# A feed-forward block whose residual adds move to transfers, and a sixth pair of row tiles in seven products

## The chip, the cores and the metric

The kernel runs on one core of one Trainium2 chip. The metric is the device time of one execution in microseconds; three runs of the kernel before gave a median of 1134.25 (1134.21 to 1136.03). A core has a matrix engine (TensorE, PE in the profile; its weight loads are PEld), a vector engine (VectorE, DVE), a scalar engine (ScalarE, ACT), a general engine (GpSimd, POOL) and an engine that issues transfers (SyncE, SP). Matrix products are summed in eight banks (each 128 x 512 float32), from which VectorE and ScalarE read. Everything else lies in on-chip tiles of 128 partitions.

## The reference

One decoder layer on 256 tokens of width 2048, all in float32. The mixers (gated linear attention and sparse attention) come first and give the residual h. The change lies in what follows, the feed-forward part, of width 5632:

```python
h = x + jnp.concatenate([gla_out, nsa_out], axis=-1) @ w_out
m = rms_norm(h, ffn_norm_g)
return h + (jax.nn.silu(m @ w_gate) * (m @ w_up)) @ w_down
```

## The kernel before

**Split products.** Each float32 operand of a large product is split into a rounded high part and a low rest, and a product is three matmuls: high by high, high by low, low by high. `in_parts` (lines 563 to 565) makes the two parts: line 564 copies the high part on ScalarE, line 565 subtracts it from the original on VectorE. Weights arrive as raw tiles of 1 MB (`fraw`, three buffers) by transfers that SyncE issues in `load4` (line 932), and their parts lie in `ftwo` tiles (four buffers, each with high and low part of up to 4 x 128 x 512 numbers).

**Stages.** After the projections, the mixers and the output projection (to about 440 us) the feed-forward part runs in eleven blocks of 512 hidden columns. In each block `gate_up` computes gate and up for both token tiles (t = 0, 1; 128 tokens each), and one block later `down` multiplies the activations by four column groups n of `w_down` and adds the result to the residual tiles `h_sb[n]` (two token tiles of 512 columns each). The order is gate_up(0), gate_up(1), down(0), gate_up(2), down(1) and so on to gate_up(10), down(9), down(10). `down(10)` is the last: it adds in halves of 256 columns and sends each half out.

**Pairs of row tiles.** The 2048 rows of the gate and up weights are 16 tiles of 128, taken in eight pairs (0 to 7). A plain pair is 8 products of 3 matmuls, 24 in all. A pair in `PAIRS7` is computed by a Strassen-like scheme with 7 products, 21 matmuls: the weights are added up first (lines 983 to 985, VectorE), the sums are split too (into a second `ftwo` buffer), and the activations are needed in four combined forms, made once by `pair_forms` after the output projection and kept in a `g4` tile for all blocks. Eight banks hold the sums, numbered 1 to 8. After the last pair of this kind banks 1, 5, 6 and 7 are combined (line 1008 on ScalarE, lines 1009 to 1012 on VectorE), and after the last pair of all the gating follows (lines 1021 to 1024): the sums from banks 2, 3, 4 and 8 are added, ScalarE applies Silu, VectorE multiplies.

**Order of the work.** The program is written in the order of the loops; `drive` interleaves side work (the transposes of the last block's activations, `turn_act`) at a set pace. A planner then orders the instructions of each engine by priority and by its own costs and hands out tile buffers. Each engine works through its own queue in that order, so what stands behind a waiting instruction waits too. Pairs run in `ORDER`: in the first block first 1 and 3, plainly, and then 0, 5, 2, 4, 6, 7; later 0, 1, 2, 4, 3, 5, 6, 7, with 1, 3 and 7 plain.

**Residual adds.** After both token tiles of a column group have been summed over the block, `down` adds them on VectorE, one instruction of 128 x 512 for each token tile (line 1055).

Of the kernel before, what the change touches and what calls it, by code (L numbers as in the profile page):

```python
# [11 lines left out]
AF = mybir.ActivationFunctionType  # L12
ALU = mybir.AluOpType
AX = mybir.AxisListType

P = 128
S = 256
NT = S // P
# [18 lines left out]
def kernel(  # L37
# [4 lines left out]
    nc = tc.nc  # L42
    act, mm = nc.scalar.activation, nc.tensor.matmul
    TT, TS, STT = nc.vector.tensor_tensor, nc.vector.tensor_scalar, nc.vector.scalar_tensor_tensor
# [12 lines left out]
    def slot(pool, tag, bufs, align=None):  # L57
        def f(shape, dt=F32):
            n_tiles[0] += 1
            return pool.tile([P] + list(shape), dt, tag=tag, bufs=bufs, name=f"{tag}_{n_tiles[0]}", align_bytes=align)  # L60
        return f
# [3 lines left out]
    g4, g2, g1, small = slot(gp, "g4", 24, LINE), slot(s2p, "g2", 13), slot(s1p, "g1", 7), slot(s1p, "sm", 12)  # L65

    def bank():
        n_tiles[0] += 1
        return pp.tile([P, 512], F32, tag="bank", name=f"bank_{n_tiles[0]}")
# [36 lines left out]
    last = {}  # L106
# [85 lines left out]
    def transpose(o, i, n=P):  # L192
        return nc.tensor.transpose(o, i, ident[:n, :n])  # L193
# [369 lines left out]
    def in_parts(hi, lo, ps):  # L563
        act(hi, ps, AF.Copy)  # L564
        TT(lo, ps, f32(hi), ALU.subtract)  # L565
# [273 lines left out]
    h_sb = []  # L839
# [22 lines left out]

    PAIRS7, FIRST7 = (0, 2, 4, 5, 6), (0, 2, 4)


    OLD = (1, 3)
    ORDER0, ORDER = OLD + (0, 5, 2, 4, 6, 7), (0, 1, 2, 4, 3, 5, 6, 7)
    forms = {}  # L870
    turned = set()

    def pair_forms(pair, v):

        f = g2([4, P])
        a0, a1, b0, b1 = v[:, 0, :P], v[:, 0, P:], v[:, 1, :P], v[:, 1, P:]
        TT(f[:, 0], b1, a1, ALU.subtract)
        TT(f[:, 1], f[:, 0], b0, ALU.subtract)
        TT(f[:, 2], b0, b1, ALU.subtract)
        TT(f[:, 3], a0, f[:, 1], ALU.add)  # L880
        r = forms[pair] = g4([2, 4, P], F32R)
        in_parts(r[:, 0], r[:, 1], f)
# [32 lines left out]
    rf = kp.tile([P, NT], F32, name="rf")  # L915
    fw = {}

    def ffn_pools():
        nonlocal g2, small
        for pool in (wp, s2p, s1p, cp):  # L920
            pool.release()
        fr = ctx.enter_context(tc.tile_pool(name="fr", bufs=1, reuse_waits="tile"))
        fs = ctx.enter_context(tc.tile_pool(name="fs", bufs=1, reuse_waits="tile"))
        fp = ctx.enter_context(tc.tile_pool(name="fp", bufs=1, reuse_waits="tile"))
        fw["raw"], fw["two"] = slot(fr, "fraw", 3, LINE), slot(fp, "ftwo", 4, LINE)
        g2, small = slot(fs, "f2", 10), slot(fs, "fm", 4)

    def load4(parts):

# [10 lines left out]
    def parts_of(src):  # L940

        if not fw:
            return split(src, 4, 512)
        n = src.shape[1]
        hi, lo = two_parts()
        in_parts(hi[:, :n], lo[:, :n], src)
        return [(hi[:, k], lo[:, k]) for k in range(n)]

    def gate_up(fb, aTs, before):

        hi, lo = g4([4, S], F32R), g4([4, S], F32R)
        aTs.append((hi, lo))
        banks = {}

        def product(q, a, w, k):

            if q not in banks:
                banks[q] = bank()
                new = True
            else:  # L960
                new = False
            for i, (x, m) in enumerate(((a[0], w[k][0]), (a[0], w[k][1]), (a[1], w[k][0]))):
                todo[q] -= 1
                mm(banks[q], x, m, start=new and i == 0, stop=todo[q] == 0)  # L964

        def tokens(k, t):
            assert k in turned
            return tuple(x[k // 4][:, k % 4, t * P:(t + 1) * P] for x in (hT_h, hT_l))

        order, sevens = (ORDER0, FIRST7) if fb == 0 else (ORDER, PAIRS7)  # L970
        last7 = max(sevens, key=order.index)
        todo = dict.fromkeys((1, 5, 6, 7), 3 * len(sevens))
        todo.update(dict.fromkeys((2, 3, 4), 3 * len(sevens) + 6 * (8 - len(sevens))))
        todo[8] = 6 * (8 - len(sevens))
        for at, pair in enumerate(order):
            if fb == 0 and at == len(OLD):
                ffn_pools()
            a, b = 2 * pair, 2 * pair + 1
            r = load4([(m[0], a, 2, fb * FB) for m in (w_gate, w_up)])
            if pair in sevens:  # L980
                w = parts_of(r[:, 0:3])
                s1, s2 = g4([2, 512]), g4([2, 512])
                TT(s1, r[:, 1:3], r[:, 3:4].to_broadcast([P, 2, 512]), ALU.add)  # L983
                TT(s2[:, 0], s1[:, 1], r[:, 1], ALU.add)  # L984
                TT(s2[:, 1], s2[:, 0], r[:, 0], ALU.add)  # L985
                f = [tuple(forms[pair][:, i, j] for i in range(2)) for j in range(4)]
                product(1, tokens(b, 0), w, 1)
                yield 2
                product(2, tokens(a, 0), w, 0)
                yield 2  # L990
                product(3, f[3], w, 2)
                yield 2
                hi_, lo_ = two_parts()
                in_parts(hi_[:, 0:2], lo_[:, 0:2], s1)
                in_parts(hi_[:, 2:4], lo_[:, 2:4], s2)
                w = [(hi_[:, k], lo_[:, k]) for k in range(4)]
                for q, x, k in ((5, f[0], 0), (7, f[2], 1), (6, f[1], 2), (4, tokens(a, 1), 3)):
                    product(q, x, w, k)
                    yield 2
            else:  # L1000
                w = parts_of(r)
                for q, t, m in ((2, 0, 0), (3, 0, 1), (4, 1, 0), (8, 1, 1)):
                    for j in range(2):
                        product(q, tokens(a + j, t), w, 2 * m + j)
                        yield 2
            if pair == last7:
                q1, u, q5u, q7u, q57u = (g2([512]) for _ in range(5))
                act(q1, banks[1], AF.Copy)
                TT(u, banks[6], q1, ALU.add)
                TT(q5u, banks[5], u, ALU.subtract)  # L1010
                TT(q7u, banks[7], u, ALU.add)
                TT(q57u, banks[5], q7u, ALU.subtract)
                if before is not None:
                    urgent.append(before)
        if fb == 0:
            drain(urgent)
            rms(rf, ssh)
            TT(rf, rf, hback, ALU.mult)
        gs = []
        for t, (g, gq, u_, uq) in enumerate(((q1, 2, q5u, 3), (q7u, 4, q57u, 8))):  # L1020
            TT(g, banks[gq], g, ALU.add)
            act(g, g, AF.Silu, scale=rf[:, t:t + 1])
            TT(u_, banks[uq], u_, ALU.add)
            STT(g, u_, rf[:, t:t + 1], g, ALU.mult, ALU.mult)
            gs.append(g)
        turns[fb] = turn_act(gs, hi, lo)

    turns = {}

    def turn_act(gs, hi, lo):  # L1030
        for t in range(NT):
            ts = slice(t * P, (t + 1) * P)
            p = bank()
            for j in range(4):
                transpose(p[:, j * P:(j + 1) * P], gs[t][:, j * P:(j + 1) * P])
                if j % 2:
                    yield
            pv = p.rearrange("p (j s) -> p j s", j=4)
            in_parts(hi[:, :, ts], lo[:, :, ts], pv)

    def down(f0, aTs, last):

        for m in range(2):
            banks = [[bank() for _ in range(NT)] for _ in range(2)]
            for f, (ah, al) in enumerate(aTs):
                end = f == len(aTs) - 1
                for i, n in enumerate((2 * m, 2 * m + 1)):
                    ws = parts_of(load4([(w_down[0], 4 * (f0 + f), 4, n * 512)]))
                    yield from chunk([banks[i]], ah, al, ws, f == 0, end, t_first=last and end)
                    if not end:  # L1050
                        continue
                    for t in range(NT):
                        for c in range(0, 512, 256 if last else 512):
                            cs = slice(c, c + (256 if last else 512))
                            TT(h_sb[n][:, t, cs], banks[i][t][:, cs], h_sb[n][:, t, cs], ALU.add)  # L1055
                            if last:
                                nc.sync.dma_start(out[t * P:(t + 1) * P, n * 512 + c:n * 512 + c + 256], h_sb[n][:, t, cs])


    drive([proj(C_LR, ev_go(0), ((0, 256), (256, 272)), first_chunk)], 2)  # L1060
# [50 lines left out]
```

## Time and profile before

| | |
|---|---|
| median of three runs | 1134.25 us |
| profiled execution | 1134.1 us, its span 1132.4 us |
| busy in the span: PE, DVE, ACT, POOL | 1120.4, 965.9, 619.8, 23.6 us |
| granted TensorE clock | 0.999 of full speed |
| moved by DMA | 213.45 MB, 189 GB/s on average |

The span is that of the profiled instructions; 1.7 us lie around it. "L1055" is line 1055 of the kernel before. A group's row names the operation, output<-input, the partitions x elements, the count, then the busy time, the mean duration and the idle time just before it with what ended that idle time. A row of a timeline has the start, the length, the engine, the line and the operation; "x2" is two instructions merged. The share "DMA" is the mean busy share of the 16 DMA engines.

### The profile page before, as it was taken

The page shows a single profiled execution, that of the slowest core. Times are in us where ns is not written, and L with a number is a line of the kernel's source. Part 1 is how long each engine was busy: PE and PEld are TensorE (multiplying, and loading weights), DVE is VectorE, ACT ScalarE, POOL GpSimd, SP SyncE. Part 2 cuts the span into 40 slices and gives each one's busy share as a digit, 9 for nine tenths or more (in the row PEclk, how much of TensorE's full clock was granted, in tenths as well). Part 3 has the DMA queues.
Part 4 walks back from the last instruction along what each step waited for, and adds up shares of the span by engine and source line. Part 5 has one row for each costly group of instructions (what it writes and reads, how often), then busy time and mean ns, then how long its engine had stood idle before and what let it go on. Part 6 is the DMA issues. An engine that isn't in the chain of part 4 may idle for free.

```text
span 1132.4 us, 14359 instructions
## 1 busy us (share of the span) xinstructions
PE 1120.4 (99%) x5515; PEld 927.1 (82%) x5515; DVE 965.9 (85%) x1205; ACT 619.8 (55%) x763; POOL 23.6 (2%) x53
## 2 busy tenths in 40 slices
PE   9999999999999999999999999999999999999998
PEld 8888889998777777788888888888888888888886
DVE  6547779987588678999999999999999999999993
ACT  7654466544466486664555546364555555464640
POOL 3000000100000000000000000000000000000000
PEclk9999999999999999999999999999999999999999
DMA  7655543445853354556665656555565556565652
GB/s 269 233 186 186 186 149 114 152 151 152 299 182 112 112 186 149 184 193 219 221 224 180 225 180 233 186 202 193 199 208 200 207 166 223 185 243 168 196 211 75
DMA packets 110446, 213.45 MB, mean 189 GB/s; under 512 B 5109, under 2 KB 8217, under 8 KB 110378
## 3 DMA queue, kind: packets, MB, share of 16 engines
q1 hardware_dynamic: 110378, 212.54, 56.1%
q8 instruction: 43, 0.70, 0.2%
q14 instruction: 25, 0.20, 0.1%
HBM read 210.42 MB, written 2.10 MB: 188 GB/s over the span
## 4 chain that ended last, share of the span: by engine, by line
PE 89%; issue 4%; DVE 4%; DMA 1%; POOL 0%; SPq 0%; ACT 0%; POOLq 0%; DVEq 0%
PE bank L261 45%; PE bank L964 37%; PE bank L193 3%; PE bank L817 1%; PE bank L759 1%; DVE ftwo L565 1%; DMA raw<-in_w_out_dram 1%; DVE lo L130 1%; DMA g<-in_x_dram 1%; PE bank L513 1%; DVE g L515 0%; DVE g L518 0%; DVE g L490 0%; PE bank L675 0%; DVE g L489 0%
## 5 line engine op out<-in xcount | busy, mean ns | idle before, releaser
L964 PE MATMUL bank<-ftwo,g 128*128 128x512 f32 x1905 | 444.9, 392 | 1.3 <-DVE ftwo L565 1.1
L964 PEld LDWEIGHTS bank<-ftwo,g 128*128 128x128 f32 x1905 | 354.0, 188 | 75.4 <-DVE ftwo L565 2.2
L261 PE MATMUL bank<-hi,g 128*128 128x512 f32 (+3 forms) x1152 | 326.3, 366 | 0.8 <-DVE g L615 0.6
L564 ACT ACTIVATE ftwo<-fraw 128x1536 fp32r<-128x1536 f32 (+1 forms) x130 | 226.3, 1741 | 141.5 <-PE bank L261 41.2
L565 DVE TENSOR_TENSOR ftwo<-fraw,ftwo 128x1536 fp32r<-128x1536 f32 (+1 forms) x130 | 267.2, 2067 | 13.8 <-ACT ftwo L564 13.8
L261 PE MATMUL bank<-ftwo,g 128*128 128x512 f32 x1056 | 241.9, 389 | 0.0
L261 PEld LDWEIGHTS bank<-ftwo,g 128*128 128x128 f32 x1056 | 198.0, 188 | 41.6 <-DVE g L565 0.4
L261 PEld LDWEIGHTS bank<-hi,g 128*128 128x128 f32 x1152 | 199.3, 189 | 30.9 <-issue 2.3
L130 DVE TENSOR_TENSOR lo<-raw,hi 128x1024 fp32r<-128x1024 f32 (+3 forms) x125 | 151.4, 1218 | 74.5 <-ACT hi L129 74.0
L564 ACT ACTIVATE ftwo<-g 128x1024 fp32r<-128x1024 f32 x106 | 110.5, 1058 | 158.9 <-DVE g L983 75.2
L261 PE MATMUL bank<-lo,g 128*128 128x512 f32 (+1 forms) x576 | 195.3, 365 | 0.5 <-DVE lo L130 0.5
L129 ACT ACTIVATE hi<-raw 128x1024 fp32r<-128x1024 f32 (+3 forms) x125 | 131.3, 1056 | 109.3 <-PE bank L261 77.5
L565 DVE TENSOR_TENSOR ftwo<-g,ftwo 128x1024 fp32r<-128x1024 f32 x106 | 127.2, 1217 | 8.2 <-ACT ftwo L564 8.2
L261 PEld LDWEIGHTS bank<-lo,g 128*128 128x128 f32 x576 | 102.6, 189 | 15.0 <-issue 0.9
L1055 DVE TENSOR_TENSOR g<-bank,g 128x512 f32<-128x512 f32 (+1 forms) x96 | 59.3, 642 | 15.6 <-PE bank L261 14.7
L983 DVE TENSOR_TENSOR g<-fraw 128x1024 f32<-128x1024 f32 x53 | 64.5, 1216 | 0.0
L564 ACT ACTIVATE g<-bank 128x512 fp32r<-128x512 f32 (+1 forms) x50 | 29.2, 587 | 21.8 <-PE bank L193 12.5
L193 PE MATMUL bank<-ident,g 128*128 128x128 f32 (+2 forms) x214 | 38.4, 278 | 2.4 <-DVE g L548 1.1
L565 DVE TENSOR_TENSOR g<-bank,g 128x512 fp32r<-128x512 f32 (+1 forms) x50 | 33.6, 681 | 7.7 <-ACT g L564 7.4
L193 PEld LDWEIGHTS bank<-ident,g 128*128 128x128 f32 (+2 forms) x214 | 27.5, 142 | 12.3 <-issue 2.3
L985 DVE TENSOR_TENSOR g<-g,fraw 128x512 f32<-128x512 f32 x53 | 36.3, 685 | 0.6
L984 DVE TENSOR_TENSOR g<-g,fraw 128x512 f32<-128x512 f32 x53 | 36.3, 685 | 0.5
(192 smaller groups left out, 639.3 us busy)
## 6 DMA issues: line engine op xcount, KB each, us to landing
fraw<-in_w_down_dram SPq DMA_DIRECT2D x44, 1024.0 KB, 5.1
fraw<-in_w_gate_dram SPq DMA_DIRECT2D x86, 512.0 KB, 3.8
fraw<-in_w_up_dram SPq DMA_DIRECT2D x86, 512.0 KB, 4.7
raw<-in_w_in_dram SPq DMA_DIRECT2D x36, 1024.0 KB, 5.1
raw<-in_w_out_dram SPq DMA_DIRECT2D x16, 1024.0 KB, 5.1
raw<-in_w_in_dram SPq DMA_DIRECT2D x4, 1072.0 KB
g<-in_x_dram SPq DMA_DIRECT2D x7, 512.0 KB, 9.8
raw<-in_w_in_dram SPq DMA_DIRECT2D x3, 1056.0 KB, 11.4
```

The costliest lines, as they stand in the source:

```text
L129: act(h[:, i:i + n], r[:, k + i:k + i + n], AF.Copy)
L130: TT(o[:, i:i + n], r[:, k + i:k + i + n], f32(h[:, i:i + n]), ALU.subtract)
L193: return nc.tensor.transpose(o, i, ident[:n, :n])
L261: last["mm"] = mm(bk[t], a[:, k, t * P:(t + 1) * P], m[:, off:off + w], start=(first_ and k == 0 and i == 0), stop=(end and k == 3 and i = ...
L513: mm(p[:, j * P:(j + 1) * P], u, w, start=True, stop=True)
L564: act(hi, ps, AF.Copy)
L565: TT(lo, ps, f32(hi), ALU.subtract)
L964: mm(banks[q], x, m, start=new and i == 0, stop=todo[q] == 0)
L983: TT(s1, r[:, 1:3], r[:, 3:4].to_broadcast([P, 2, 512]), ALU.add)
L984: TT(s2[:, 0], s1[:, 1], r[:, 1], ALU.add)
L985: TT(s2[:, 1], s2[:, 0], r[:, 0], ALU.add)
L1055: TT(h_sb[n][:, t, cs], banks[i][t][:, cs], h_sb[n][:, t, cs], ALU.add)
```

## The change

Three things are changed together.

1. In `down`, for all blocks but the last, ScalarE copies the two sums of a column group from the banks into a tile `step` (two buffers, 128 x 2 x 512 each), and one transfer issued from GpSimd adds the tile to `h_sb[n]`. VectorE's adds stay only in the last block.
2. From the third block on six pairs (0, 1, 2, 4, 5, 6) are in seven products, with the order 0, 1, 3, 2, 4, 5, 6, 7. The second block has four such pairs (0, 2, 4, 5) in the order 0, 1, 2, 3, 4, 6, 5, 7; the first is as before. `pair_forms` makes the forms of pair 1 as well.
3. The small tiles of the feed-forward part are arranged anew in the same space: in place of ten buffers `f2` of 512 columns there are two `gate` buffers, one `up` buffer (each two token tiles of 512) and the two of `step`. The combined sums are written into parts of `gate` and `up`.

```diff
-    PAIRS7, FIRST7 = (0, 2, 4, 5, 6), (0, 2, 4)
+    PAIRS7, FIRST7 = (0, 1, 2, 4, 5, 6), ((0, 2, 4), (0, 2, 4, 5))
...
-    ORDER0, ORDER = OLD + (0, 5, 2, 4, 6, 7), (0, 1, 2, 4, 3, 5, 6, 7)
+    ORDERS, ORDER = (OLD + (0, 5, 2, 4, 6, 7), (0, 1, 2, 3, 4, 6, 5, 7)), (0, 1, 3, 2, 4, 5, 6, 7)
...
-        f = g2([4, P])
+        f = fw["up"]([4, P]) if fw else g2([4, P])
...
-        g2, small = slot(fs, "f2", 10), slot(fs, "fm", 4)
+        fw["up"], fw["step"] = slot(fs, "up", 1), slot(fs, "step", 2)
+        g2, small = slot(fs, "gate", 2), slot(fs, "fm", 4)
...
-        order, sevens = (ORDER0, FIRST7) if fb == 0 else (ORDER, PAIRS7)
+        order, sevens = (ORDERS[fb], FIRST7[fb]) if fb < 2 else (ORDER, PAIRS7)
...
-                q1, u, q5u, q7u, q57u = (g2([512]) for _ in range(5))
-                act(q1, banks[1], AF.Copy)
-                TT(u, banks[6], q1, ALU.add)
-                TT(q5u, banks[5], u, ALU.subtract)
-                TT(q7u, banks[7], u, ALU.add)
-                TT(q57u, banks[5], q7u, ALU.subtract)
+
+                gate, up = g2([NT, 512]), fw["up"]([NT, 512])
+                act(gate[:, 0], banks[1], AF.Copy)
+                TT(up[:, 1], banks[6], gate[:, 0], ALU.add)
+                TT(up[:, 0], banks[5], up[:, 1], ALU.subtract)
+                TT(gate[:, 1], banks[7], up[:, 1], ALU.add)
+                TT(up[:, 1], banks[5], gate[:, 1], ALU.subtract)
...
+                    if not last:
+                        step = fw["step"]([NT, 512])
+                        for t in range(NT):
+                            act(step[:, t], banks[i][t], AF.Copy)
+                        nc.gpsimd.dma_start(h_sb[n], step, accum_op=ALU.add)
+                        continue
                     for t in range(NT):
-                        for c in range(0, 512, 256 if last else 512):
-                            cs = slice(c, c + (256 if last else 512))
+                        for c in range(0, 512, 256):
+                            cs = slice(c, c + 256)
                             TT(h_sb[n][:, t, cs], banks[i][t][:, cs], h_sb[n][:, t, cs], ALU.add)
-                            if last:
-                                nc.sync.dma_start(out[t * P:(t + 1) * P, n * 512 + c:n * 512 + c + 256], h_sb[n][:, t, cs])
+                            nc.sync.dma_start(out[t * P:(t + 1) * P, n * 512 + c:n * 512 + c + 256], h_sb[n][:, t, cs])
```

More of the change, by code (lines that the diff above doesn't have):

```diff
@@ L1018, in gate_up, with turn_act @@
             TT(rf, rf, hback, ALU.mult)
-        gs = []
-        for t, (g, gq, u_, uq) in enumerate(((q1, 2, q5u, 3), (q7u, 4, q57u, 8))):
+        for t, (gq, uq) in enumerate(((2, 3), (4, 8))):
+            g, u = gate[:, t], up[:, t]
             TT(g, banks[gq], g, ALU.add)
             act(g, g, AF.Silu, scale=rf[:, t:t + 1])
[L1023 to L1026, printed above, removed]
+            TT(u, banks[uq], u, ALU.add)
+            STT(g, u, rf[:, t:t + 1], g, ALU.mult, ALU.mult)
+        turns[fb] = turn_act(gate, hi, lo)
     turns = {}
-    def turn_act(gs, hi, lo):
+    def turn_act(gate, hi, lo):
         for t in range(NT):
@@ L1034, in turn_act @@
             for j in range(4):
-                transpose(p[:, j * P:(j + 1) * P], gs[t][:, j * P:(j + 1) * P])
+                transpose(p[:, j * P:(j + 1) * P], gate[:, t, j * P:(j + 1) * P])
                 if j % 2:
```

## The prediction

> **What bounds the kernel now.** I read the page's busy line first, then the chain that ended last in order of time, then the windows of one block of the feed-forward part, then who waited for whom. The page, and rows of the chain (start, length, engine, line):
>
> ```profile
> PE 1120.4 (99%) x5515; PEld 927.1 (82%) x5515; DVE 965.9 (85%) x1205; ACT 619.8 (55%) x763; POOL 23.6 (2%) x53
> ...
> PE 89%; issue 4%; DVE 4%; DMA 1%; POOL 0%; SPq 0%; ACT 0%; POOLq 0%; DVEq 0%
> ```
>
> ```profile
> 642.48 21.76 PE bank L261 x96
> 664.25 36.04 PE bank L964 x159
> ...
> 705.33 21.76 PE bank L261 x96
> ```
>
> From about 440 us on the chain is TensorE alone, back to back. A block lasts 705.33 - 642.48 = 62.85 us: 96 down products, 177 gate and up products (159 of them in the row shown), eight transposes. One product costs 21.76 / 96 = 0.2267 us. The windows (length, then busy time of PE, PEld, DVE, ACT and POOL, granted clock, DMA share, GB/s) tell how close the others are:
>
> ```profile
> 375.00:440.00 65.00, 64.29 (x302) 51.93 (x301) 43.84 (x71) 46.19 (x76) 1.39 (x2) 1.00 0.46 162
> 440.00:516.80 76.80, 75.45 (x330) 60.34 (x329) 75.93 (x72) 46.43 (x39) 0.00 (x0) 1.00 0.60 201
> ```
>
> ```profile
> 642.40:705.30 62.90, 62.90 (x283) 51.98 (x282) 60.17 (x58) 33.78 (x27) 0.00 (x0) 1.00 0.61 202
> ```
>
> TensorE is never idle in a steady block, at full granted clock. VectorE is second, 60.17 of 62.90 us: 2.7 us free. ScalarE has 29 us free and GpSimd all. VectorE's waits, summed over nine blocks (516.8 to 1082.7 us), and TensorE's between 380 and 516 us:
>
> ```profile
> DVE ftwo L565 <- ACT ftwo L564: 18.8, 32, 1.2
> ```
>
> ```profile
> PE bank L964 <- DVE ftwo L565: 1.1, 2, 0.8
> ```
>
> VectorE's idle time is no lateness of its own: it waits for ScalarE's first half of a split, and ScalarE, as shown below, waits for TensorE to give a split buffer back. So TensorE bounds, and a product removed is worth 0.2267 us as long as VectorE keeps its lead.
>
> **The change, part by part.** *Products on TensorE.* A pair of row tiles takes 24 products plainly and 21 in seven products. From the third block on six pairs of eight are in seven, before five: 3 fewer in each of 9 blocks. The second block has four pairs where it had five: 3 more. The first keeps its three. Together 27 - 3 = 24 products, 24 x 0.2267 = 5.44 us off TensorE. The down product's matmuls stay.
>
> *VectorE.* Its groups in the block 642.4 to 705.3 us (instructions, busy us, mean ns):
>
> ```profile
> L565 DVE TENSOR_TENSOR ftwo<-fraw,ftwo 128x2048 fp32r<-128x2048 f32 x7 | 16.0, 2284 | 1.0 <-ACT ftwo L564 1.0
> L565 DVE TENSOR_TENSOR ftwo<-g,ftwo 128x1024 fp32r<-128x1024 f32 x10 | 11.9, 1216 | 1.2 <-ACT ftwo L564 1.2
> L565 DVE TENSOR_TENSOR ftwo<-fraw,ftwo 128x1536 fp32r<-128x1536 f32 x5 | 8.7, 1750 | 0.3 <-ACT ftwo L564 0.3
> L983 DVE TENSOR_TENSOR g<-fraw 128x1024 f32<-128x1024 f32 x5 | 6.1, 1215 | 0.0
> L1055 DVE TENSOR_TENSOR g<-bank,g 128x512 f32<-128x512 f32 x8 | 5.3, 685 | 0.2
> L985 DVE TENSOR_TENSOR g<-g,fraw 128x512 f32<-128x512 f32 x5 | 3.4, 686 | 0.1
> L984 DVE TENSOR_TENSOR g<-g,fraw 128x512 f32<-128x512 f32 x5 | 3.4, 684 | 0.0
> ```
>
> A pair turned from plain to seven adds 1.750 + 2 x 1.216 + 1.215 + 0.684 + 0.686 - 2.284 = 4.48 us; the eight residual adds taken away give 8 x 0.685 = 5.48. Net -1.0 by means; consecutive instructions overlap by some 0.08 us (two of 1.216 last 2.35 in the timeline below), which makes it -0.76. So 59.4 us of work stand in a block of 62.90 - 0.68 = 62.2 us: 2.8 us free, as now. VectorE doesn't become the bound on average.
>
> *ScalarE.* Its groups in the same block:
>
> ```profile
> L564 ACT ACTIVATE ftwo<-fraw 128x2048 fp32r<-128x2048 f32 x7 | 13.4, 1917 | 4.8 <-DMA fraw<-in_w_down_dram 2.3 <-PE bank L964 1.3 <-PE bank L261 1.1
> L564 ACT ACTIVATE ftwo<-g 128x1024 fp32r<-128x1024 f32 x10 | 10.4, 1059 | 15.9 <-PE bank L964 8.9 <-DVE g L983 5.8 <-DVE g L985 1.1
> L564 ACT ACTIVATE ftwo<-fraw 128x1536 fp32r<-128x1536 f32 x5 | 7.4, 1489 | 7.9 <-PE bank L261 3.5 <-issue 2.9 <-PE bank L964 0.8
> ...
> L1008 ACT ACTIVATE f<-bank 128x512 f32<-128x512 f32 x1 | 0.6, 580 | 0.0
> ```
>
> The pair adds 1.489 + 2 x 1.059 - 1.917 = 1.69 us, the eight copies from the banks 8 x 0.580 = 4.64 (that row is such a copy). 33.78 + 6.3 = 40.1 of 62.2: free on average. But behind a copy stand ScalarE's splits, and behind those VectorE's and TensorE. So the lead has to be walked.
>
> *The lead in the gate and up stage.* Three timelines (start, length, engine):
>
> ```profile
> 658.89 1.92 ACT L564 ACTIVATE ftwo<-fraw 128x2048 fp32r<-128x2048 f32 x1 [1.12 <-PE bank L261]
> 664.33 1.49 ACT L564 ACTIVATE ftwo<-fraw 128x1536 fp32r<-128x1536 f32 x1 [3.52 <-PE bank L261]
> ```
>
> ```profile
> 664.08 36.21 PE L964 MATMUL bank<-ftwo,g 128*128 128x512 f32 x159
> ```
>
> ```profile
> 676.15 2.35 DVE L565 TENSOR_TENSOR ftwo<-g,ftwo 128x1024 fp32r<-128x1024 f32 x2
> ...
> 679.02 3.95 DVE L565 TENSOR_TENSOR ftwo<-fraw,ftwo 128x2048 fp32r<-128x2048 f32 x2
> ```
>
> There are four split buffers, and both waits end as TensorE finishes a down product (one at 664.08 - 5.44, one at 664.08). Today's tightest place: the fourth and fifth pairs. After pairs of 21, 24 and 21 products TensorE has run 66 x 0.2267 = 14.96 us, so it starts the fourth at 679.04 and, after its 21, the fifth at 683.80; that one's split ends at 679.02 + 2.2 = 681.2: a lead of 2.6 us. Now the new order (pairs 0, 1, 3, 2, 4, 5, 6, 7, with 3 and 7 plain), time from the stage's start, a seven-product pair taking 2.04 us from its first buffer and 2.72 from its second: the four-buffer rule lets pair 1's buffers begin at -5.44 and 0, pair 3's at 2.04, pair 2's at 4.76 and 6.80, pair 4's at 9.52 and 14.96, 5's at 17.0 and 19.7, 6's at 21.8 and 24.5, 7's at 26.5. With ScalarE's and VectorE's times above in that order, VectorE finishes pair 1's second half at 3.2 (4.3 with the last two copies in front; needed at 6.80), pair 3 at 6.2 (7.2; 9.52), pair 4's second half at 18.3 (21.76), pair 6's first and second at 27.0 and 29.3 (29.24 and 31.28), pair 7 at 31.5 (34.0). The lead shrinks to about 2 us where it was 2.6, and stays positive: I book no stall. Were that cover gone, each us of lateness would cost TensorE that us in every block.
>
> *The transfers that add.* Four a block, 40 in all, of 512 KB between on-chip tiles, issued from GpSimd's queue, where nothing else stands after 440 us. No such transfer is in the trace. Nearest rows:
>
> ```profile
> fraw<-in_w_gate_dram SPq DMA_DIRECT2D x86, 512.0 KB, 3.8
> ...
> g<-in_x_dram SPq DMA_DIRECT2D x7, 512.0 KB, 9.8
> ```
>
> ```profile
> GB/s 385 166 42 0 0 0 0 0 0 0 72 102 344 400 415 415 215 15 113 245 396 347 351 359 68 38 0 0 53 143 328 396 415 396 200 0 0 0 0 0
> ```
>
> The last line cuts 642.4 to 664.1 us in 40: loads come in bursts of up to 415 GB/s, with gaps. One transfer read twice (its source and what it adds to) is 1.05 MB, 2.5 us at that rate; four are 10 us of the 0.39 x 62.2 = 24.3 us that the engines have free. From below: nothing, they sit in the gaps. From above: 9.8 us each, 39 us, which overfills the block by 15 us. I take 2.5 to 5 us and no cost, since the gate rows (3.8) carry the same bytes in this very stage, the x rows only at the crowded start. The two copy tiles are reused two products later, 10.9 us: only a transfer beyond some 9 us holds ScalarE back. The last block adds on VectorE again: to each quarter of the residual three down products, 16.3 us, after that quarter's last transfer can start; the tail keeps its length.
>
> *GpSimd beside VectorE.* In the first 10 us the trace shows the two in each other's way:
>
> ```profile
> 6.98 0.44 POOL L347 TENSOR_SCALAR_AFFINE_SELECT lmask<-lmask 128x64 f32<-128x64 f32 x2
> ...
> 7.47 1.28 POOL L347 TENSOR_SCALAR_AFFINE_SELECT lmask<-lmask 128x64 f32<-128x64 f32 x2
> ```
>
> ```profile
> 1.65 1.07 DVE L368 CAST identb<-ident 128x128 bf16<-128x128 f32 x1 [0.46 <-POOL ident masks.py:199]
> ...
> 7.14 1.50 DVE L130 TENSOR_TENSOR lo<-raw,hi 128x528 fp32r<-128x528 f32 x2
> ...
> 17.06 0.28 DVE L367 CAST cneg<-g 128x256 bf16<-128x256 f32 x1
> ```
>
> Two selects take 1.28 us instead of 0.44 beside a two-operand subtraction, which itself isn't slowed (1.50 for two); and a cast takes 1.07, when one twice its size takes 0.28, at the time of GpSimd's long memset. So an issue could cost VectorE anything from 0 to 0.8 us. I take 0: the stage has two-operand operations alone, and beside those GpSimd was the one to wait. The Trainium skill ("SBUF — State Buffer", section "Who interferes with whom") says that a VectorE instruction with two SBUF inputs contends with a GpSimd instruction that reads SBUF, and not with one that only writes it; by that rule writing a transfer's descriptors costs VectorE nothing and the sum stays as it is, by the cast's row it would be the second rival's. The rows of the selects agree with the rule; none here shows an issue from GpSimd.
>
> *The rest, with one answer.* The forms of pair 1, four small subtractions and additions and one split more, fall before 440 us, where VectorE has 65 - 43.8 = 21 us free: 0. The four combinations and the gating keep their operations under other tile names; the single "up" tile is read out a stage before it is written again: 0. One more kept form leaves 24 - 18 = 6 big tiles for two split inputs a pair and two activations: 0. Between 440 and 516.8 us VectorE is full (75.93 of 76.80) and one pair less in the second block takes 4.5 us off it; the 1.1 us that TensorE waited there could shrink; I take 0, because the longer wait stands at the head of that block, before the pair that changes:
>
> ```profile
> 479.75 29.30 PE L964 MATMUL bank<-ftwo,g 128*128 128x512 f32 x127 [0.80 <-DVE ftwo L565]
> ```
>
> **Sum.** The profiled execution took 1134.1 us (span 1132.4), the median 1134.25: the same within 0.02%. 1134.1 - 5.44 = 1128.7 us, 0.5% faster. Below 0.2% (2.3 us) a run can't be told from no change.
>
> **The rivals.**
> (1) *Crowded transfers*, slower. Speaks for it: DMA is 0.61 busy, in bursts; against: 24 us free a block. It decides from 24.3 / 4 = 6.1 us of all engines per transfer; at 6.5 a block grows by 1.7 us, in ten blocks 17: 1128.7 + 17 = 1146; at 9.8 a block grows by 15 us: 1278.
> (2) *GpSimd's issues block VectorE*, slower. With the cast's 0.8 us, 4 x 0.8 = 3.2 against 2.8 free: 0.4 a block, 4 us: 1132.7; from (2.8 + 0.54) / 4 = 0.84 us an issue all the gain is gone, at 1.2 it is 1128.7 + 20 = 1149. For: the cast's row; against: the select's.
> (3) *The lead runs dry*, no change. Should the planner not start pair 1 as early as the walk, the 2 us are overrun and TensorE waits 0.6 us a block: 1134.
> (4) *A copy too early in ScalarE's queue*, slower. A pair of copies queued one product ahead of its sums holds the split behind it for up to 5.44 us, 3.4 more than the lead: ten times is 34 us, 1163; with 3 us it is 1 us a block, 1139. It decides from 2.6 us. For: ScalarE already waits for TensorE's banks; against: VectorE's own adds waited only 0.2 us in the block shown, so the order fits TensorE's pace.
>
> **How the numbers follow.** Forecast 0.60 (own range 1127.5 to 1131.5: a us gained in the second block, a few stalls); crowded 0.13; issues 0.11; lead 0.06; copies 0.10. Faster: 0.60 and a quarter of the issues' 0.11, less what the forecast's upper end loses, 0.61. Same: the lead and some of the issues, 0.08. Slower: the rest, 0.31. The range goes from 1127.3 to 1142: it holds the forecast, the lead, most of the issues and the mild ends of copies and crowding.
>
> **What would show it.** Right: blocks of 62.2 us in the chain, TensorE alone, the second one 0.7 us longer; VectorE's L1055 group left with the last block's 16 halves; ScalarE near 40 us a block; transfers landing within 9 us. Wrong: TensorE waiting for "ftwo" in each block (lead, copies), DMA share near 1 with waits for "fraw" (crowded), VectorE's means above 2.28 and 1.22 us (issues), ScalarE waiting for a transfer out of "step".

## The result, and the profile after

The changed kernel takes 1151.83 us (median of four runs, 1144.97 to 1155.52) against 1135.03 for the kernel before in the same comparison: 1.0141 times, interval 1.0091 to 1.0191. It is slower by about 1.4%, where 0.5% faster was forecast. The profiled execution took 1153.2 us, its span 1151.4, which is 19.0 us more than the span before.

The page of the changed kernel, its busy line, queues, chain and transfers:

```profile
PE 1121.0 (97%) x5491; PEld 919.8 (80%) x5491; DVE 948.1 (82%) x1170; ACT 673.9 (59%) x860; POOL 58.0 (5%) x93
...
q1 hardware_dynamic: 110378, 212.54, 54.3%
q0 software_dynamic: 5760, 20.97, 9.5%
...
PE 51%; DVE 25%; DMA 13%; issue 9%; ACT 1%; SPq 1%; POOL 0%; DVEq 0%; ACTq 0%; POOLq 0%
...
fraw<-in_w_gate_dram SPq DMA_DIRECT2D x86, 512.0 KB, 4.5
fraw<-in_w_up_dram SPq DMA_DIRECT2D x86, 512.0 KB, 5.7
...
g<-step POOLq DMA_DIRECT2D x40, 512.0 KB, 7.6
```

The 24 products are gone (5515 to 5491 matmuls), yet the chain is no longer TensorE's: VectorE has 25% of it and DMA 13%, where they had 4% and 1%. The loads of `w_up` land after 5.7 us instead of 4.7. The new queue q0 carries the transfers that add: they take 9.5% of 16 engines over 1151.4 us, so 109 us for 40, or 2.73 us of all engines each.

Starts of the down products in TensorE's timeline:

```profile
517.36 21.92 PE L261 MATMUL bank<-ftwo,g 128*128 128x512 f32 x96
583.65 22.09 PE L261 MATMUL bank<-ftwo,g 128*128 128x512 f32 x96
...
713.92 22.13 PE L261 MATMUL bank<-ftwo,g 128*128 128x512 f32 x96
776.81 21.99 PE L261 MATMUL bank<-ftwo,g 128*128 128x512 f32 x96
...
903.00 22.21 PE L261 MATMUL bank<-ftwo,g 128*128 128x512 f32 x96
969.52 22.33 PE L261 MATMUL bank<-ftwo,g 128*128 128x512 f32 x96
```

The blocks are not all alike. The three that begin at 517.36, 713.92 and 903.00 last 66.3, 62.9 and 66.5 us; the nine between 517.36 and 1101.58 us last 584.2 together, 24.7 more than nine of the 62.17 that the products alone give. 24.7 - 5.4 saved = 19.3, against 19.0 measured: the whole difference is in these blocks. Who waited for whom from 440 us on, first TensorE, then VectorE:

```profile
PE bank L965 <- DVE ftwo L565: 18.3, 20, 3.0
```

```profile
DVE g L984 <- DMA fraw<-in_w_up_dram: 41.8, 17, 5.3
DVE ftwo L565 <- ACT ftwo L564: 21.1, 14, 3.1
```

TensorE waits for splits, and VectorE, ahead of them, for late loads: line 984 (983 before) is the first sum of a pair's weights. One long block shows the sequence. SyncE, VectorE and TensorE (the gate and up stage starts at 925):

```profile
917.51 1.05 SPq L933 DMA_DIRECT2D fraw<-in_w_up_dram  x1
```

```profile
927.41 1.22 DVE L984 TENSOR_TENSOR g<-fraw 128x1024 f32<-128x1024 f32 x1 [3.84 <-DMA fraw<-in_w_up_dram]
928.67 0.69 DVE L985 TENSOR_TENSOR g<-g,fraw 128x512 f32<-128x512 f32 x1
929.39 0.69 DVE L986 TENSOR_TENSOR g<-g,fraw 128x512 f32<-128x512 f32 x1
930.00 2.35 DVE L565 TENSOR_TENSOR ftwo<-g,ftwo 128x1024 fp32r<-128x1024 f32 x2
934.25 1.23 DVE L984 TENSOR_TENSOR g<-fraw 128x1024 f32<-128x1024 f32 x1 [1.90 <-DMA fraw<-in_w_up_dram]
935.39 3.95 DVE L565 TENSOR_TENSOR ftwo<-fraw,ftwo 128x2048 fp32r<-128x2048 f32 x2
```

```profile
937.73 23.46 PE L965 MATMUL bank<-ftwo,g 128*128 128x512 f32 x102 [2.78 <-DVE ftwo L565]
```

The load issued at 917.51 reaches VectorE 9.9 us later. The sums that need it, those of pair 2, stand at the head of VectorE's queue, and behind them the second half of pair 1 (930.00). In this block that half comes just in time; in the blocks from 583.65, 969.52 and 1035.36 TensorE waits 0.35 to 0.48 us for it. Behind the next late sums (934.25) stands pair 3 (935.39), for which TensorE waits 2.78 us here.

The length of a block follows this wait of VectorE around the end of the down stage. Three more rows, from the blocks that begin at 583.65, 713.92 and 776.81:

```profile
609.25 1.22 DVE L984 TENSOR_TENSOR g<-fraw 128x1024 f32<-128x1024 f32 x1 [5.14 <-DMA fraw<-in_w_up_dram]
...
736.45 1.22 DVE L984 TENSOR_TENSOR g<-fraw 128x1024 f32<-128x1024 f32 x1 [2.03 <-DMA fraw<-in_w_up_dram]
...
798.83 1.23 DVE L984 TENSOR_TENSOR g<-fraw 128x1024 f32<-128x1024 f32 x1 [1.67 <-DMA fraw<-in_w_up_dram]
```

| first wait for the load of pair 2 | 1.67 | 2.03 | 2.55 | 3.40 | 5.14 | 5.26 | 5.28 us |
|---|---|---|---|---|---|---|---|
| length of the block | 62.8 | 62.9 | 63.4 | 64.2 | 66.0 | 65.8 | 66.2 us |

These are the seven blocks with one wait above 1 us; the other two, from 517.36 and 903.00, have a second one and last 66.3 and 66.5. Against the 62.17 us of the products the first 1.0 to 1.6 us of the wait cost nothing; every further microsecond costs about one.

The windows of these microseconds in the block from 903.00, columns as in the prediction:

```profile
914.00:919.40 5.40, 5.40 (x26) 4.46 (x25) 5.37 (x7) 3.12 (x5) 0.86 (x1) 1.00 1.05 290
919.40:924.90 5.50, 5.50 (x26) 4.57 (x25) 2.85 (x3) 2.63 (x4) 0.85 (x1) 1.00 1.05 301
924.90:930.00 5.10, 5.10 (x24) 4.24 (x23) 2.52 (x3) 4.61 (x5) 0.86 (x1) 1.00 1.06 308
```

For 16 us the DMA engines are full (a share above 1 means that the times of packets overlap). In the kernel before their share in the same part of a block, from 11 to 27 us after its start, was

```profile
653.10:669.10 16.00, 16.00 (x73) 13.23 (x72) 15.53 (x17) 7.45 (x6) 0.00 (x0) 1.00 0.55 188
```

so 0.45 x 16.0 = 7.2 us were free, and the four transfers, issued from 7 to 23 us after the start, ask for 4 x 2.73 = 10.9.

### The profile page after: what moved, and what is told of

It is laid out like the page before. It is cut to its first block, busy times and chain, and to the rows that moved or that the text cites. A ratio compares the mean times of both kernels' runs of the same rounds, so it can differ in the third digit from the quotient of the medians.

```text
span 1151.4 us, 14498 instructions
## 1 busy us (share of the span) xinstructions
PE 1121.0 (97%) x5491; PEld 919.8 (80%) x5491; DVE 948.1 (82%) x1170; ACT 673.9 (59%) x860; POOL 58.0 (5%) x93
## 4 chain that ended last, share of the span: by engine, by line
PE 51%; DVE 25%; DMA 13%; issue 9%; ACT 1%; SPq 1%; POOL 0%; DVEq 0%; ACTq 0%; POOLq 0%
PE bank L261 34%; DVE ftwo L565 15%; DMA fraw<-in_w_up_dram 11%; PE bank L965 10%; DVE g L984 3%; PE bank L193 3%; DVE g L986 2%; DVE g L985 1%; PE bank L817 1%; ACT ftwo L564 1%; PE bank L759 1%; DMA raw<-in_w_out_dram 1%; DVE lo L130 1%; PE bank L513 1%; DMA raw<-in_w_in_dram 1%
## 5 line engine op out<-in xcount | busy, mean ns | idle before, releaser
L965 PEld LDWEIGHTS bank<-ftwo,g 128*128 128x128 f32 x1881 | 348.2, 188 | 98.1 <-DVE ftwo L565 27.0
L565 DVE TENSOR_TENSOR ftwo<-fraw,ftwo 128x1536 fp32r<-128x1536 f32 (+1 forms) x130 | 262.9, 2033 | 21.1 <-ACT ftwo L564 21.1
L564 ACT ACTIVATE ftwo<-fraw 128x1536 fp32r<-128x1536 f32 (+1 forms) x130 | 222.2, 1709 | 50.8 <-DMA fraw<-in_w_down_dram 19.9
L261 PEld LDWEIGHTS bank<-ftwo,g 128*128 128x128 f32 x1056 | 197.4, 188 | 43.6 <-DVE g L565 2.7
L564 ACT ACTIVATE ftwo<-g 128x1024 fp32r<-128x1024 f32 x122 | 127.0, 1056 | 119.3 <-DVE g L986 47.8
L565 DVE TENSOR_TENSOR ftwo<-g,ftwo 128x1024 fp32r<-128x1024 f32 x122 | 146.2, 1217 | 0.0
L984 DVE TENSOR_TENSOR g<-fraw 128x1024 f32<-128x1024 f32 x61 | 74.4, 1220 | 42.1 <-DMA fraw<-in_w_up_dram 41.8
L1056 ACT ACTIVATE step<-bank 128x512 f32<-128x512 f32 x80 | 47.8, 598 | 86.1 <-PE bank L261 83.9
L1057 POOL DMA_DIRECT2D g<-step x40 | 34.5, 863 | 652.3 <-ACT step L1056 652.3
L985 DVE TENSOR_TENSOR g<-g,fraw 128x512 f32<-128x512 f32 x61 | 41.8, 686 | 0.7
L986 DVE TENSOR_TENSOR g<-g,fraw 128x512 f32<-128x512 f32 x61 | 41.7, 684 | 0.4
```

What stands on the lines that cost most here:

```text
L261: last["mm"] = mm(bk[t], a[:, k, t * P:(t + 1) * P], m[:, off:off + w], start=(first_ and k == 0 and i == 0), stop=(end and k == 3 and i = ...
L1056: act(step[:, t], banks[i][t], AF.Copy)
L1057: nc.gpsimd.dma_start(h_sb[n], step, accum_op=ALU.add)
```

## The experiments

**Theories.** Crowding: the transfers fill the engines during the down stage, loads land late, and VectorE's queue passes the delay on. Rival: the sixth pair, with ScalarE's copies, runs the lead dry by itself. Every run is compared with the kernel before on the same chip (its medians 1134.25 to 1135.35); edits are against the changed kernel unless another is named.

### Each part alone

```diff
-                        step = fw["step"]([NT, 512])
                         for t in range(NT):
-                            act(step[:, t], banks[i][t], AF.Copy)
-                        nc.gpsimd.dma_start(h_sb[n], step, accum_op=ALU.add)
+                            TT(h_sb[n][:, t], banks[i][t], h_sb[n][:, t], ALU.add)
```

> The changed kernel with the residual adds back on VectorE and no transfers: the sixth pair alone. Both theories see VectorE as the bound here: 60.2 + 4.1 = 64.3 us of work for 62.2 us of TensorE, so up to 9 x 2.1 = 19 us over the 1128.7 that TensorE alone would give: 1135 to 1148 us. Late loads (crowding theory): VectorE waits for no fraw load. A time above that of the changed kernel would say that the transfers are still the better half.

Measured 1153.22 us, 1.0164 (1.0149 to 1.0179): above the expected range. Six pairs without relief for VectorE are as slow as the change. A window of 66 us of it:

```profile
650.00:716.00 66.00, 64.63 (x286) 52.28 (x285) 64.89 (x65) 35.11 (x30) 0.00 (x0) 1.00 0.56 192
```

VectorE has 1.1 us free in 66, the DMA share is only 0.56, and VectorE never waits for a load: here VectorE is the bound, at blocks of mostly 64.7 us. The sixth pair needs the adds off VectorE.

```diff
-    PAIRS7, FIRST7 = (0, 1, 2, 4, 5, 6), ((0, 2, 4), (0, 2, 4, 5))
+    PAIRS7, FIRST7 = (0, 2, 4, 5, 6), ((0, 2, 4), (0, 2, 4, 5, 6))
...
-    ORDERS, ORDER = (OLD + (0, 5, 2, 4, 6, 7), (0, 1, 2, 3, 4, 6, 5, 7)), (0, 1, 3, 2, 4, 5, 6, 7)
+    ORDERS, ORDER = (OLD + (0, 5, 2, 4, 6, 7), (0, 1, 2, 4, 3, 5, 6, 7)), (0, 1, 2, 4, 3, 5, 6, 7)
```

> The transfers alone: pairs and orders as in the kernel before (five pairs in seven products from the second block on). Crowding theory (the transfers make weight loads land late): transfers land after 7 to 8 us and loads late as in the changed kernel, but VectorE has 7.5 us a block to spare instead of 2.8, so a part of the stalls stays: 1136 to 1143 us. Rival (the sixth pair's lead is too short whatever the transfers do): no stall, 1134 to 1135 us.

Measured 1142.31 us, 1.0070 (1.0055 to 1.0085). The transfers alone cost 8 us although VectorE has 4.5 us a block less to do. TensorE's and VectorE's waits:

```profile
PE bank L965 <- DVE ftwo L565: 7.8, 11, 1.4
```

```profile
DVE g L984 <- DMA fraw<-in_w_up_dram: 54.7, 22, 4.1
```

The rival, which had no stall here, falls as the whole cause.

### The transfers taken away, or made plain copies

```diff
-                        nc.gpsimd.dma_start(h_sb[n], step, accum_op=ALU.add)
```

> The changed kernel without the 40 transfers; ScalarE's copies stay, the residual adds of all blocks but the last are left out. Crowding theory: no late loads, TensorE back to back, 1128 to 1130 us, blocks of 62.2 us. Rival (the sixth pair or the copies in ScalarE's queue run the lead dry by themselves): 1145 to 1155 us as with the transfers.

Measured 1128.49 us, 0.9948 (0.9932 to 0.9965), the time that the prediction's sum had for the whole change. Its waits, and a block:

```profile
DVE g L984 <- DMA fraw<-in_w_up_dram: 5.0, 9, 1.8
```

```profile
641.40:703.60 62.20, 62.20 (x279) 51.37 (x278) 58.73 (x55) 39.55 (x37) 0.00 (x0) 1.00 0.59 203
```

Blocks of 62.2 us without a gap: the sixth pair, the new order, the small tiles and the copies in ScalarE's queue work as walked. All the loss hangs on the transfers.

```diff
-                        nc.gpsimd.dma_start(h_sb[n], step, accum_op=ALU.add)
+                        nc.gpsimd.dma_start(h_sb[n], step)
```

> The changed kernel with each transfer as a plain copy from the step tile over the residual tile, issued at the same place of GpSimd's queue: the same issues and bytes written, one read of the residual less, so the residual adds are lost. If it is the DMA engines' time that crowds the loads: each transfer takes 1.3 to 1.6 us of all engines where the adding one takes 2.7, and the time falls to between 1129 and 1142 us. If an issue from GpSimd or any second stream of transfers does the harm: 1145 to 1155 us.

Measured 1129.01 us, 0.9955 (0.9938 to 0.9971). A second stream from GpSimd does no harm by itself. The queue and the landing:

```profile
q0 software_dynamic: 5760, 20.97, 4.6%
...
g<-step POOLq DMA_DIRECT2D x40, 512.0 KB, 4.4
```

A plain copy of the same 512 KB takes 4.6% x 1126.4 / 40 = 1.30 us of all engines and lands after 4.4 us. The adding one took 2.73 and 7.6: about twice, as for bytes that are read twice.

To see whether the engine time or the adding itself does the harm, the plain copy was made twice, one after the other:

```diff
-                        nc.gpsimd.dma_start(h_sb[n], step, accum_op=ALU.add)
+                        nc.gpsimd.dma_start(h_sb[n], step)
+                        nc.gpsimd.dma_start(h_sb[n], step)
```

> The plain copy made twice, one after the other, from the same step tile over the same residual tile: the same engine time as the adding transfer (2 x 1.3 = 2.6 us against 2.7) and no addition (the residual adds are lost). If engine time is what crowds the loads: 1140 to 1155 us, VectorE waiting some 40 us for the loads of w_up. If it is something in the adding itself (each engine held while it reads the residual and writes it back): 1128.5 to 1133 us, the loads landing as with one plain copy.

Measured 1149.38 us, 1.0130 (1.0106 to 1.0153): the loss is back, but not by the expected way alone. ScalarE now waited for the step tiles, which two copies in a row hold for longer, and VectorE waited for loads only 11.6 us. Waits of ScalarE and VectorE from 440 to 1090 us:

```profile
ACT step L1056 <- DMA g<-step: 48.3, 15, 6.6
```

```profile
DVE g L984 <- DMA fraw<-in_w_up_dram: 11.6, 11, 3.3
```

So another run had three step tiles:

```diff
-    g4, g2, g1, small = slot(gp, "g4", 24, LINE), slot(s2p, "g2", 13), slot(s1p, "g1", 7), slot(s1p, "sm", 12)
+    g4, g2, g1, small = slot(gp, "g4", 23, LINE), slot(s2p, "g2", 13), slot(s1p, "g1", 7), slot(s1p, "sm", 12)
...
-        fw["up"], fw["step"] = slot(fs, "up", 1), slot(fs, "step", 2)
+        fw["up"], fw["step"] = slot(fs, "up", 1), slot(fs, "step", 3)
```

> Two plain copies one after the other as before, with three step tiles so that ScalarE does not wait for them (the space comes from one big tile; the residual adds are lost). 2.6 us of engine time a group and no wait for step. If the engines' time alone delays the loads: 1140 to 1155 us, TensorE stalled behind VectorE's waits for w_up. If the loss of the run with two copies came from ScalarE's wait for the step tile: 1129 to 1134 us.

Measured 1149.32 us, 1.0125 (1.0110 to 1.0140). The two copies together take 2.84 us of all engines (q0 has 9.9% of 1147.5 us for 80). ScalarE waits for a step tile only once (3.1 us), and VectorE waits for loads nearly as much as in the changed kernel:

```profile
DVE g L984 <- DMA fraw<-in_w_up_dram: 35.8, 26, 3.6
```

Engine time without any adding delays the loads and costs nearly the same. The one big tile fewer can't be the reason: two fewer make the kernel faster (below).

### Less crowding, or earlier loads

```diff
+                        if n % 2:
+                            step = fw["step"]([NT, 512])
...
+                            continue
+                        for t in range(NT):
+                            TT(h_sb[n][:, t], banks[i][t], h_sb[n][:, t], ALU.add)
+                        continue
```

> The changed kernel with two of the four column groups (0 and 2) added on VectorE and two (1 and 3) by transfers. Crowding: half the transfers' engine time, but 2.4 us more on VectorE a block, 61.8 of 62.2 us: 1131 to 1142 us. If any transfer at this place is enough to spoil a block: 1145 to 1155 us.

Measured 1130.06 us, 0.9959 (0.9944 to 0.9974). This is just below the range expected under crowding. With two transfers a block instead of four VectorE waits for loads 1.9 us in all, never longer than 0.8, and with two column groups back it still keeps up:

```profile
DVE g L984 <- DMA fraw<-in_w_up_dram: 1.9, 3, 0.8
```

```diff
-    g4, g2, g1, small = slot(gp, "g4", 24, LINE), slot(s2p, "g2", 13), slot(s1p, "g1", 7), slot(s1p, "sm", 12)
+    g4, g2, g1, small = slot(gp, "g4", 22, LINE), slot(s2p, "g2", 13), slot(s1p, "g1", 7), slot(s1p, "sm", 12)
...
-        fw["raw"], fw["two"] = slot(fr, "fraw", 3, LINE), slot(fp, "ftwo", 4, LINE)
+        fw["raw"], fw["two"] = slot(fr, "fraw", 4, LINE), slot(fp, "ftwo", 4, LINE)
```

> The changed kernel with four raw weight buffers for three (the space comes from two of the 24 big tiles). If loads that land late are the cause, a load can start a buffer earlier, some 5 us, more than VectorE's longest wait for one: 1128 to 1134 us. If the engines are simply full over the whole block, or the two tiles fewer bind, it stays at 1140 to 1155 us.

Measured 1128.12 us, 0.9947 (0.9932 to 0.9962): faster than both kernels, with all adds by transfers. Its largest waits of VectorE, and a block:

```profile
DVE ftwo L565 <- ACT ftwo L564: 15.2, 21, 0.9
DVE g L984 <- PE bank L261: 13.0, 9, 1.4
```

```profile
643.80:706.00 62.20, 62.20 (x280) 51.43 (x279) 59.00 (x55) 39.58 (x38) 3.44 (x4) 1.00 0.76 237
...
654.80:670.80 16.00, 16.00 (x73) 13.25 (x72) 12.85 (x14) 10.21 (x12) 2.58 (x3) 1.00 1.04 294
```

The engines are as full as in the changed kernel in the same part of a block (1.04, second row), the transfers take as much of them (q0 9.6%), and the loads of `w_up` still land after 5.7 us; but no load is late any more. The load that was late, the fourth of a block's eight, is now issued 8.3 us after the block's start (714.29 in the block from 705.99) instead of some 14.5. Two controls belong to it. The first has the two big tiles fewer and three raw buffers:

```diff
-    g4, g2, g1, small = slot(gp, "g4", 24, LINE), slot(s2p, "g2", 13), slot(s1p, "g1", 7), slot(s1p, "sm", 12)
+    g4, g2, g1, small = slot(gp, "g4", 22, LINE), slot(s2p, "g2", 13), slot(s1p, "g1", 7), slot(s1p, "sm", 12)
```

> The changed kernel with 22 of the 24 big tiles and three raw buffers: the control for the four raw buffers. If the fourth raw buffer made the gain: 1145 to 1156 us, as the changed kernel. If the smaller number of big tiles did it, by holding the sums of the next pair back: 1128 to 1135 us.

Measured 1137.25 us (seven runs, 1133.42 to 1142.23), 1.0026 (1.0003 to 1.0049). Neither expectation holds: fewer big tiles alone give back a good part of the loss. VectorE waits for late loads 17.9 us in six waits where it had 41.8 in 17:

```profile
DVE g L984 <- DMA fraw<-in_w_up_dram: 17.9, 6, 5.2
```

Four of its waits before pair sums (6.0 us) now end with TensorE's down product, presumably because the sums' big tile is still read there. What is left of the loss still comes from late loads. In the profiled execution (1141.85 us) the six blocks in which no load is later than 2.04 us last 62.1 to 62.5 us; the three with waits of 2.96, 5.23 and 5.24 us last 63.5, 65.9 and 66.1. Why fewer tiles make a load late in fewer blocks was not tested. The fourth raw buffer then brings the rest, from 1.0026 to 0.9947.

The second control is the kernel before with four raw buffers and 22 big tiles (the same two edits).

> The kernel before with four raw buffers and 22 big tiles: the control for what the fourth buffer gives without the change. TensorE is already back to back from 440 us on: within 0.2% of 1134.3 us by either theory. Faster by more would mean that the run with four buffers owes its gain to the buffers and not to the products.

Measured 1135.73 us, 1.0003 (0.9994 to 1.0013): nothing. The gain of the four-buffer version over the kernel before is that of the 24 products.

### The order of the sums

`in_parts` returns its subtraction and the last one of each pair is kept in `last["lo"]`; `behind` puts what follows after it in VectorE's queue:

```diff
+                split_before = last.get("lo")
                 w = parts_of(r[:, 0:3])
...
+                with behind(split_before):
-                TT(s1, r[:, 1:3], r[:, 3:4].to_broadcast([P, 2, 512]), ALU.add)
+                    TT(s1, r[:, 1:3], r[:, 3:4].to_broadcast([P, 2, 512]), ALU.add)
...
-                in_parts(hi_[:, 2:4], lo_[:, 2:4], s2)
+                last["lo"] = in_parts(hi_[:, 2:4], lo_[:, 2:4], s2)
```

> The changed kernel with one rule more for VectorE's queue: the sums of a pair's weights stand behind the last split of the pair before, so a load that is late holds only its own pair. Transfers and loads unchanged. If the harm is done by the sums that wait at the head of VectorE's queue with a ready split behind them: the stalls of 1.5 to 3.0 us at the second and third pair go, 1130 to 1142 us. If the loads are late for their own pairs already: 1145 to 1155 us.

Measured 1176.36 us, 1.0353 (1.0328 to 1.0378): worse than the changed kernel by another 2%, and above both expected ranges. VectorE's waits for loads are gone (0.3 us), and ScalarE's and VectorE's for each other have grown:

```profile
ACT ftwo L564 <- DVE g L986: 120.9, 36, 5.7
```

```profile
DVE ftwo L565 <- ACT ftwo L564: 62.3, 51, 3.7
```

The early sums let ScalarE copy them in time. Strictly pair after pair, ScalarE's copy, VectorE's subtraction and the next sums follow each other with gaps. So forbidding the early sums is no cure. That a late load at the head of the queue passes the delay on rests on the long block and the nine lengths above; this run loses time in another way and can't tell.

### The adds on GpSimd

```diff
-                        nc.gpsimd.dma_start(h_sb[n], step, accum_op=ALU.add)
+                        nc.gpsimd.tensor_tensor(h_sb[n], step, h_sb[n], ALU.add)
```

> The changed kernel with each transfer replaced by one addition on GpSimd from the step tile (128 x 1024): no extra traffic on the DMA engines, but GpSimd reads two tiles beside VectorE. Crowding theory alone: no late loads, 1128 to 1131 us. If GpSimd and VectorE hold each other up (the prediction's second rival), VectorE's means rise above 2.28 and 1.22 us, and four long additions a block against 2.8 us free give 1135 to 1160 us.

Measured 1186.73 us, 1.0455 (1.0437 to 1.0474), above both expected ranges. GpSimd's and VectorE's groups from 600 to 1100 us:

```profile
L1057 POOL TENSOR_TENSOR g<-step,g 128x1024 f32<-128x1024 f32 x32 | 119.7, 3760 | 427.0 <-ACT step L1056 427.0
```

```profile
L565 DVE TENSOR_TENSOR ftwo<-fraw,ftwo 128x1536 fp32r<-128x1536 f32 x43 | 97.5, 2267 | 0.0
L984 DVE TENSOR_TENSOR g<-fraw 128x1024 f32<-128x1024 f32 x45 | 72.5, 1610 | 4.3 <-DMA fraw<-in_w_up_dram 4.2
L986 DVE TENSOR_TENSOR g<-g,fraw 128x512 f32<-128x512 f32 x45 | 48.6, 1080 | 0.3
```

VectorE's means of these groups rise from 1.75 to 2.27, from 1.22 to 1.61 and from 0.68 to 1.08 us, and VectorE becomes the bound, busy 493.5 of 500 us. The means hide how long single instructions are held. One place, first GpSimd, then VectorE:

```profile
729.89 9.95 POOL L1057 TENSOR_TENSOR g<-step,g 128x1024 f32<-128x1024 f32 x2 [48.38 <-ACT step L1056]
```

```profile
734.82 2.78 DVE L985 TENSOR_TENSOR g<-g,fraw 128x512 f32<-128x512 f32 x1
737.52 3.41 DVE L984 TENSOR_TENSOR g<-fraw 128x1024 f32<-128x1024 f32 x1
```

An addition that takes 0.69 us elsewhere takes 2.78 here, and one of 1.22 takes 3.41; two additions on GpSimd take 9.95 us here and 5.75 us at 743.73.

## Why the prediction was wrong, point by point

- *Products on TensorE, 5.44 us.* Right. Without the transfers the gain is 1134.25 - 1128.49 = 5.8 us, and with four raw buffers 1128.12 us is reached with the transfers as well.
- *VectorE 59.4 and ScalarE 40.1 us a block.* Right: 58.7 and 39.6 in the run without transfers, 59.0 and 39.6 with four raw buffers.
- *The lead.* The walk holds while loads are on time, as the run without transfers shows. The cover was near its size, 1.0 to 1.6 us in the seven blocks where the walk had about 2, and beyond it each microsecond of lateness cost about one, as the prediction said. TensorE's waits in the nine blocks stand after 31, 43 or 145 matmuls of the gate and up stage, that is, one matmul into pair 1's second half, into pair 3 or into the last sums of pair 6. The last is where the walk had its least lead, 2.0 us. What it left out is a load that lands later: it took each raw tile as there, although the sums of pair 2 stand in VectorE's queue ahead of splits that are due.
- *The transfers that add: the step that failed.* Their size was right, 2.73 us of all engines (2.5 to 5 were taken) and 7.6 us to landing (within 9). They were set against the 24.3 us that the engines have free in a whole block. They are all issued within some 16 us around the down stage, where 7.2 us were free for 10.9, and the load of pair 2, issued in that stage, reaches VectorE 7.7 to 11.3 us after issue. So the cost that the prediction put at nothing was 24.7 us over nine blocks. "They sit in the gaps" was true of the block and false of the stage. The rival "crowded transfers" named the mechanism, and the sign it gave (a DMA share near 1 with waits for "fraw") is what the trace shows. But its point of decision, 6.1 us a transfer, had the same flaw: with three raw buffers 2.73 was enough, and two plain copies of 2.84 together too.
- *GpSimd beside VectorE.* Right for the issues: in the changed kernel VectorE's means from 600 to 1100 us are 2.281, 1.216 and 1.220 us, as before, though each issue keeps GpSimd 0.86 us. The second rival didn't happen. It does happen when GpSimd reads tiles: the Trainium skill ("SBUF — State Buffer", section "Who interferes with whom") says that a VectorE instruction with two SBUF inputs contends with a GpSimd instruction that reads SBUF; the means of the run with GpSimd's additions agree. The prediction read from the selects that GpSimd is the one to wait beside two-operand instructions; in that run VectorE waits too.
- *Another queue is no relief.* The Trainium skill ("DMA: Bandwidth & Descriptors", section "Issuing engines are not separate DMA queues") says that transfers from all issuing engines share the same 16 DMA engines and interleave. The traces agree: a share of 1.05 for 16 us with both queues at work, and w_up's landing 5.7 us instead of 4.7.
- *The other rivals.* The lead running dry by itself and a copy too early in ScalarE's queue are excluded by the run with copies and no transfers.

Open is why the same load comes later in some blocks than in others. The load of `w_up` that is issued 7.5 us before the gate and up stage reaches VectorE after 8.1 us in the block from 713.92, after 9.9 us in the one from 903.00, and the engines are as full in both. No run varied that. Open is also how 22 big tiles alone bring the time down to 1137 us.

## What to carry to other kernels

Price a new transfer against the DMA time that is free in the stage where it lands, and then ask which queue has an instruction that waits for a load at its head and what is due behind it. Here moving work off a full engine onto transfers paid when the loads had one more buffer of lead, or when only half of it was moved: 2.73 us each, four times in 16 us, made the kernel 1151.8 us with three raw buffers and 1128.1 with four (and two big tiles fewer); twice in a block it was 1130.1 with three. When two parts are changed at once, the run that leaves out the moved work's carrier, copies without transfers here, tells in one step which of them costs.

## What the runs showed of the hardware

A transfer that adds 512 KB between on-chip tiles takes 2.73 us of all 16 DMA engines and 7.6 us to land in this traffic, a plain one 1.30 and 4.4. Its issue keeps GpSimd 0.863 us, a plain one 0.543. An addition of 128 x 1024 on GpSimd beside a busy VectorE takes 3.76 us on average and lengthens the mean of one group of VectorE's two-operand additions of 128 x 512 from 0.68 to 1.08 us, and single ones to 2.78.
